# Two transformer blocks on one core: memory keys projected in float32, modulation sums placed behind steps, and 512-column weight chunks

## The chip, the cores and the metric

The kernel runs on one core of a Trainium2 chip. The metric is the device time of one execution in microseconds (us); the runs shown are whole executions, and a profiled execution carries a trace beside its time. PE is the matmul engine, PEld its weight loads, DVE the vector engine, ACT the scalar engine, POOL the GpSimd engine, SP the engine whose queue issues most loads.

## The reference, cut to what matters

The input `x` has 512 tokens of 1024 columns, all in float32. Two blocks follow one another, and beside them lies a memory of 256 rows.

```python
# block 1
mod = silu(c) @ w_ada + b_ada; shift, scale, gate = split(mod, 3)
h = rms_norm(x, g_pre) * (1 + scale) + shift
qa, ka, va, fa, za, qb, kb, vb, zb = split(h @ w_in)
oa = forgetting_attention(qa, ka, va, fa + b_fgate) * silu(za)      # 8 heads of 64, "fox"
ob = window_sink_attention(rope(qb), rope(kb), vb, sinks) * silu(zb)  # window 128, 2 key heads, "swa"
x = x + gate * rms_norm(concat(oa, ob) @ w_out, g_post)
# block 2
h = rms_norm(x, norm_g); mem_h = rms_norm(mem, mem_norm_g)
glu, cgate, dq, dk, dv, dg, xq, xg, merge = split(h @ w_in_2)
y = sig(m0)*conv_branch(glu, cgate) + sig(m1)*diff_attention(dq, dk, dv, dg) \
    + sig(m2)*memory_attention(xq, xg, split(mem_h @ w_mem_kv, 2))
x = x + y @ w_out_2
```

The memory attention norms its keys per head of 256 and multiplies by a gain; only `mem`, not `x`, enters keys and values.

## The kernel before, in words

The Python program is unrolled into one list of instructions for each engine. A planner orders it: it takes instructions by priority (`low(by)` moves a priority, `after(a, b)` puts one behind another on its engine), looks for those that its own timing holds to be ready, and lets a tile be written when a buffer of its tag is free. So a load on SP can wait for a buffer, and what comes behind it in SP's queue waits too.

**Matmuls in two halves.** Operands are split into a rounded part and a rest: `load_w` (L160) loads a chunk of 256 columns and 1024 rows in two loads of 512 KB, ACT casts each of four pieces of 512 elements a partition into `wh` (L169), and DVE subtracts it from the raw weights to give `wl` (L171); the last of four pieces goes to POOL. Four `wh` and four `wl` buffers, each half a chunk, hold two chunks. The tokens stand the same way in `hh` and `hl`. Three matmuls (high-high, high-low, low-high) then stand for one. `mm_T` (L190) streams 512 tokens against stationary weights; `mm_N` (L199) streams 256 weight columns against stationary tokens, 128 tokens `t` at a time.

**The opening** (L325 to L419). The memory is loaded and transposed on PE into `mh` and `ml` (L350 to L355). Then a loop runs over the eight chunks of `w_mem`: four for the keys `mk`, four for the values. In between, the tokens are loaded (L379, in the buffers that the memory leaves), normed and transposed (L386 to L392), and eight modulation sums run: `gemv_load` (L310) loads 1 MB into one of two `ada` buffers, `gemv` (L317 to L320) multiplies and adds on DVE in nine operations into `acc` (two buffers), and `ada(k)` sums it over the partitions by two tiny matmuls (L367), adds on DVE (L368, L369), and makes `hh[k]` and `hl[k]` on ACT and POOL (L371 to L373). `ADA_LOAD` and `ADA_DO` name the chunk at which each is loaded and done. The rotary angles (L424 to L436, sine tables on ACT) and some small constants (L439 to L451) are bound behind the last modulation sum. At a lower priority (`LOWMK`) the memory keys are normed (L457 to L463), transposed by 16 transposes (L468), and stored as `kT_d` (L472).

**After it.** w1c (264 columns: window keys, window values, forget gates) and qb0 are projected at once; everything else is cut into generators ("units" end at a `yield`) that `Fill` hands out between steps of attention: `staged` runs scores, transposes and values of an attention as a pipeline, and calls for `k` units after each step. The window stage takes zb0, qb1, zb1, va0, qk0 and za0; the fox stage qk1, va1, gate, qk2, za1 and qk3. Then come w_out (two halves of the tokens, each over four chunks), the second block with `ORDER2` as the list of its units, the depthwise convolution on DVE (L904), the cross stage with the memory (`xkv`, L1085, reads `kT_d` and `v_d`), the three branches, and w_out2 in four chunks. PSUM has three `mm` banks.

## Time and profile before

| | us |
|---|---|
| runs shown | 1193.62, 1193.22, 1196.0 (median 1193.62) |
| profiled execution, its own time | 1196.61 |
| its span, first to last instruction | 1194.8 |
| PE busy | 1154.0 |
| DVE busy | 926.6 |
| ACT busy | 551.7 |
| POOL busy | 213.3 |
| mean granted PE clock | 0.991 |

The busy time of PE counts a matmul from its start to its modelled end, and matmuls overlap, so the distance from start to start is the cost of one in a dense stretch. The granted clock (PEclk) is 1.00 at 2.4 GHz and 0.50 at 1.2 GHz. An idle time of an engine is followed by the engine and line that ended it.

### The profile page before, as it was taken

To read this page: it belongs to the slowest core of one execution; us is meant where nothing else is said; L and a number is where in the kernel's file an instruction comes from. 1 tells how busy PE (TensorE), PEld (TensorE's weight loads), DVE (VectorE), ACT (ScalarE), POOL (GpSimd) and SP (SyncE) were. 2 spreads that over 40 slices of the span, in tenths; PEclk is the share of its full clock that TensorE was granted. 3 is DMA by queue.
4 is the path that set the end of the run, shared out by engine and by line. 5 is a ranking of instruction groups with operands and counts; after the bars stand their busy time and mean duration, and the time that the engine had idled before them with its cause. 6 is when DMAs were issued, how large, how long until landed. Compare 5 with 4: busy or idle time off the path is not lost.

```text
span 1194.8 us, 18995 instructions
## 1 busy us (share of the span) xinstructions
PE 1154.0 (97%) x6960; PEld 1015.9 (85%) x6960; DVE 926.6 (78%) x2055; ACT 551.7 (46%) x1173; POOL 213.3 (18%) x161
## 2 busy tenths in 40 slices
PE   7879999999989999999999999999999999999998
PEld 6878887878889988998999887988888888888898
DVE  6997777898686699999989999999692596543341
ACT  7646566557554354445554452544422354232230
POOL 1334200000112211120111221221010132011020
PEclk9989999999999999999999999999999999999999
DMA  8765312443463423324233343333446755433232
GB/s 336 259 212 164 105 56 87 152 148 110 150 231 131 124 71 98 106 89 115 89 116 106 124 141 106 106 116 106 152 147 227 267 186 185 132 97 101 86 123 79
DMA packets 61965, 165.43 MB, mean 138 GB/s; under 512 B 7120, under 2 KB 15568, under 8 KB 60848
## 3 DMA queue, kind: packets, MB, share of 16 engines
q1 hardware_dynamic: 36560, 122.41, 32.5%
q10 hardware_dynamic: 25312, 41.82, 10.0%
q8 instruction: 55, 0.90, 0.3%
q14 instruction: 38, 0.31, 0.1%
HBM read 136.80 MB, written 20.58 MB: 132 GB/s over the span
## 4 chain that ended last, share of the span: by engine, by line
PE 63%; DVE 24%; issue 3%; ACT 1%; DMA 0%; POOL 0%; ACTq 0%; DVEq 0%; POOLq 0%
PE mm L190 40%; PE mm L199 15%; DVE cv L904 7%; DVE wl L171 3%; DVE dp L1025 1%; PE pv L773 1%; DVE dp L1032 1%; PE tp L751 1%; DVE dp L1031 1%; DVE ptl L754 1%; PE sc L1157 1%; PE pv L694 1%; PE pv L1200 1%; DVE qs L259 1%; PE tp L266 1%
## 5 line engine op out<-in xcount | busy, mean ns | idle before, releaser
L169 ACT CAST wh<-raw 128x512 fp32r<-128x512 f32 x372 | 215.3, 620 | 217.7 <-PE mm L190 96.2
L171 POOL TENSOR_TENSOR wl<-raw,wh 128x512 fp32r<-128x512 f32 (+1 forms) x93 | 141.8, 1525 | 831.9 <-ACT wh L169 668.8
L171 DVE TENSOR_TENSOR wl<-raw,wh 128x512 fp32r<-128x512 f32 (+1 forms) x279 | 201.7, 747 | 95.3 <-ACT wh L169 94.9
L190 PE MATMUL mm<-hh,wh 128*128 128x512 f32 x640 | 255.9, 400 | 0.0
L190 PE MATMUL mm<-hh,wl 128*128 128x512 f32 x640 | 251.8, 393 | 0.0
L190 PE MATMUL mm<-hl,wh 128*128 128x512 f32 x640 | 251.7, 393 | 0.0
L199 PE MATMUL mm<-wh,hh 128*128 128x256 f32 (+1 forms) x672 | 193.5, 289 | 0.2 <-ACT hh L824 0.2
L904 DVE SCALAR_TENSOR_TENSOR cv<-u,vec,cv 128x512 f32<-128x512 f32 x240 | 191.1, 796 | 3.4
L199 PE MATMUL mm<-wl,hh 128*128 128x256 f32 (+1 forms) x672 | 190.7, 284 | 0.3 <-POOL wl L171 0.3
L199 PE MATMUL mm<-wh,hl 128*128 128x256 f32 (+1 forms) x672 | 190.8, 284 | 0.0
L190 PEld LDWEIGHTS mm<-hh,wl 128*128 128x128 f32 x640 | 120.5, 188 | 27.0
L190 PEld LDWEIGHTS mm<-hh,wh 128*128 128x128 f32 x640 | 120.6, 188 | 24.7
L190 PEld LDWEIGHTS mm<-hl,wh 128*128 128x128 f32 x640 | 120.8, 189 | 24.5
L199 PEld LDWEIGHTS mm<-wl,hh 128*128 128x128 f32 x672 | 128.5, 191 | 0.8 <-POOL wl L171 0.6
L199 PEld LDWEIGHTS mm<-wh,hh 128*128 128x128 f32 x672 | 127.9, 191 | 0.8 <-ACT hh L824 0.5
L199 PEld LDWEIGHTS mm<-wh,hl 128*128 128x128 f32 x672 | 128.3, 191 | 0.0
L190 PE MATMUL mm<-bh,wh 128*128 128x512 f32 x192 | 75.9, 396 | 0.0
L190 PE MATMUL mm<-bh,wl 128*128 128x512 f32 x192 | 75.4, 393 | 0.0
L190 PE MATMUL mm<-bl,wh 128*128 128x512 f32 x192 | 75.4, 393 | 0.0
L1027 ACT ACTIVATE dp<-dp,dst 128x128 f32<-128x128 f32 (+3 forms) x64 | 35.5, 556 | 54.8 <-DVE dst L1025 54.6
L199 PE MATMUL mm<-wl,mh 128*128 128x256 f32 x128 | 39.3, 307 | 6.5 <-DVE wl L171 6.5
L190 PEld LDWEIGHTS mm<-bl,wh 128*128 128x128 f32 x192 | 36.1, 188 | 8.4 <-issue 0.2
(326 smaller groups left out, 2122.4 us busy)
## 6 DMA issues: line engine op xcount, KB each, us to landing
raw<-in_w_dram SPq DMA_DIRECT2D x120, 512.0 KB
raw<-in_w_out_dram SPq DMA_DIRECT2D x24, 512.0 KB
raw<-in_w_mem_dram SPq DMA_DIRECT2D x16, 512.0 KB
ada<-in_w_ada_dram SPq DMA_DIRECT2D x8, 1024.0 KB
ada<-in_w_gate_dram SPq DMA_DIRECT2D x8, 512.0 KB
k<-ks SPq DMA_DIRECT2D x32, 128.0 KB
o_d<-sph ACTq DMA_DIRECT2D x16, 256.0 KB
o_d<-spl ACTq DMA_DIRECT2D x16, 256.0 KB
```

The costliest lines, as they stand in the source:

```text
L169: act.copy(out=wh[:, s], in_=raw[:, s])
L171: eng.tensor_tensor(out=wl[:, s], in0=raw[:, s], in1=f(wh[:, s]), op=ALU.subtract)
L190: m = pe.matmul(out=ps, lhsT=a[:, c0:c0 + P], rhs=at(b, k), start=(n == 0 and i == 0), stop=(n == KT - 1 and i == 2))
L199: pe.matmul(out=ps, lhsT=at(a, k)[:, t * P:(t + 1) * P], rhs=b[:, 0:n], start=(start and m == 0 and i == 0), stop=(stop and m == len(order ...
L259: dve.scalar_tensor_tensor(out=s[b], in0=ps[a], scalar=sc, in1=f(s[a]), op0=ALU.mult, op1=ALU.subtract)
L266: pe.transpose(out=ps[:, t * P:(t + 1) * P], in_=src[:, t, c0:c0 + P], identity=ident)
L694: pe.matmul(out=pv4[0:64], lhsT=l_, rhs=r_[:, j], start=(cnt == 0), stop=(cnt == 3 * nk - 1))
L751: pe.transpose(out=tp[:, j * P:(j + 1) * P], in_=pt_[:, j * P:(j + 1) * P], identity=ident)
L754: dve.tensor_tensor(out=ptl[:, 0:n + 1, n * P:w], in0=tv, in1=f(pth[:, 0:n + 1, n * P:w]), op=ALU.subtract)
L773: pe.matmul(out=pv[0:64, j * P:], lhsT=l_, rhs=r_[:, j, j * P:], start=(j == 0 and i == 0), stop=(j == NT - 1 and i == 2))
L904: dve.scalar_tensor_tensor(out=a, in0=u[:, j:j + S], scalar=dw[:, m * 31 + j:m * 31 + j + 1], in1=a, op0=ALU.mult, op1=ALU.add)
L1027: act.activation(out=p_[:, :w], in_=p_[:, :w], func=AF.Exp, scale=-1.0, bias=st_[:, 0, n, m:m + 1], accum_out=st_[:, 1, n, m:m + 1])
```

## The change

- `load_w` can load 512 columns: four loads of 512 KB with two row blocks `k` each, eight pieces of one `k`; `wh` and `wl` have eight buffers of half the old size; `on_pool` names the pieces of four that POOL subtracts. `mm_W` is the loop over such a chunk: `k` outside, the tokens of two (or one) PSUM banks inside, with a `yield` after every second `k`.
- qb, va, dq with dk (as dqk), xq, w_out, w_out2 and the memory's value columns become chunks of 512. The rest stays at 256.
- The opening is a straight list: loads of the memory, the first key chunk and the tokens (each in buffers of its own); rotary angles; memory transposes into one float32 tile `mT`; the first key chunk (`mem_k`, plain float32 operands, one matmul instead of three, no split); token norm and transposes; the second key chunk; `mT` split into `mh` (ACT) and `ml` (POOL) in the tokens' old buffer; two value chunks (`mem_v`, half of the `wl` pieces on POOL). Each `ada(k, step)` is bound behind a step of PE: `steps` holds one matmul for each `k` of these four chunks, 0 to 31.
- The small constants get a raised priority. The memory keys are no longer transposed there; they are stored as `k_d`, and `xkv` transposes them, four transposes for a head, two ACT evictions with the gain and two DVE operations in place of one POOL operation.
- qb is projected whole before the window stage; the window stage takes zb0, zb1, qk0, za0 and za1, the fox stage va (both halves), qk1, gate, qk2 and qk3. The second xq chunk covers heads 2 and 3, `cross_pro(1)` comes ahead of the cross stage, which calls for four units after its first two steps.

The diff, cut to its core:

```diff
-    def load_w(src, w=CW, rp=None):
-        halves = []
-        for q in range(2):
-            raw = rp.tile([P, 4, w], F32, tag="raw", name="raw", bufs=4) if rp else wp.tile([P, 4, w], F32, tag="raw", name="raw", bufs=3)
-            nc.sync.dma_start(out=raw, in_=src[:, 4 * q:4 * q + 4, :])
-            wh = wp.tile([P, 4, w], F32R, tag="wh", name="wh", bufs=4)
-            wl = wp.tile([P, 4, w], F32R, tag="wl", name="wl", bufs=4)
...
+    def load_w(src, w=CW, rp=None, order=None, on_pool=(3,)):
+        kq = 4 if w == CW else 2
+        got = {}
+        for n, q in enumerate(order or range(KT // kq)):
+            raw = rp.tile([P, kq, w], F32, tag="raw", name="raw", bufs=4) if rp else wp.tile([P, kq, w], F32, tag="raw", name="raw", bufs=3)
+            nc.sync.dma_start(out=raw, in_=src[:, kq * q:kq * q + kq, :])
             for j in range(2):
-                s = slice(2 * j, 2 * j + 2)
-                act.copy(out=wh[:, s], in_=raw[:, s])
-                eng = pool if q and j else dve
-                eng.tensor_tensor(out=wl[:, s], in0=raw[:, s], in1=f(wh[:, s]), op=ALU.subtract)
-            halves.append((wh, wl))
-        return [(halves[k // 4][0][:, k % 4, :], halves[k // 4][1][:, k % 4, :]) for k in range(KT)]
+                h = kq // 2
+                s = slice(h * j, h * (j + 1))
+                wh = wp.tile([P, h, w], F32R, tag="wh", name="wh", bufs=8)
+                wl = wp.tile([P, h, w], F32R, tag="wl", name="wl", bufs=8)
+                act.copy(out=wh, in_=raw[:, s])
+                eng = pool if (2 * n + j) % 4 in on_pool else dve
+                eng.tensor_tensor(out=wl, in0=raw[:, s], in1=f(wh), op=ALU.subtract)
+                for k in range(h):
...
+
+    def mm_W(banks, w, xh, xl, ts, order=range(KT), n=NW):
+
+        for m, k in enumerate(order):
+            wh, wl = w[k]
+            for ps, t in zip(banks, ts):
+                for i, (a, b) in enumerate(((xh, wh), (xh, wl), (xl, wh))):
+                    pe.matmul(out=ps, lhsT=at(a, k)[:, t * P:(t + 1) * P], rhs=b[:, 0:n], start=(m == 0 and i == 0), stop=(m == KT - 1 and i == 2))
+            if m % 2 and m < KT - 1:
+                yield
...
-        mt = pa.tile([P, 2, 1024], F32, tag="nat2", name="mt")
...
+        xn = pa1.tile([P, NT, 1024], F32, tag="xn", name="xn")
...
+        def raw_chunk(c, qs):
+            for q in qs:
+                r = pa.tile([P, 2, NW], F32, tag="rawm", name="rawm", bufs=6)
+                nc.sync.dma_start(out=r, in_=A["w_mem"][c][:, 2 * q:2 * q + 2, :])
+                raws[c].append(r)
...
         for t in range(2):
             nc.sync.dma_start(out=mt[:, t, :], in_=A["mem"][t])
...
+        raw_chunk(0, range(4))
+        for t in range(NT):
+            nc.sync.dma_start(out=xn[:, t, :], in_=A["xn"][t])
...
+        pf = pa1.tile([P, NT], F32, name="pf")
+        dve.tensor_copy(out=pf, in_=posi)
...
+        act.activation(out=sn, in_=ang, func=AF.Sin)
+        act.activation(out=cn, in_=rn, func=AF.Sin, scale=-1.0, bias=halfpi)
...
-                act.activation(out=mh[:, k + j, :], in_=pj, func=AF.Copy, scale=g)
-                dve.scalar_tensor_tensor(out=ml[:, k + j, :], in0=pj, scalar=g, in1=f(mh[:, k + j, :]), op0=ALU.mult, op1=ALU.subtract)
...
+                if j:
+                    dve.tensor_scalar(out=mT[:, k + j, :], in0=pj, scalar1=g, scalar2=None, op0=ALU.mult)
+                else:
+                    act.activation(out=mT[:, k + j, :], in_=pj, func=AF.Copy, scale=g)
...
+        def mem_k(c):
+            banks = [mm_tile() for t in range(2)]
+            for k in range(KT):
+                for t in range(2):
+                    m = pe.matmul(out=banks[t], lhsT=mT[:, k, t * P:(t + 1) * P], rhs=raws[c][k // 2][:, k % 2, :], start=(k == 0), stop=(k == KT - 1))
+                steps.append(m)
+            for t in range(2):
+                act.activation(out=mk[:, t, c * NW:(c + 1) * NW], in_=banks[t], func=AF.Copy, scale=mrs[:, t:t + 1])
+
+        def mem_v(c, w):
+            banks = [mm_tile() for t in range(2)]
+            for k in range(KT):
+                for t in range(2):
+                    for i, (a, b) in enumerate(((mh, w[k][0]), (mh, w[k][1]), (ml, w[k][0]))):
+                        m = pe.matmul(out=banks[t], lhsT=a[:, k, t * P:(t + 1) * P], rhs=b, start=(k == 0 and i == 0), stop=(k == KT - 1 and i == 2))
+                steps.append(m)
...
+        def ada(k, step):
...
+                m = pe.matmul(out=pm[:, j:j + 1], lhsT=acc[:, j * P:(j + 1) * P], rhs=ones[:, 0:1], start=True, stop=True)
+                if j == 0:
+                    after(m, steps[step])
...
-        adas, marks = [], {}
-        for c in range(8):
-            w = load_w(A["w_mem"][c], rp=pa)
-            if c == 1:
-                load_x()
-            adas += [gemv_load(pa, A["w_ada"][k], 256, 2) for k in ADA_LOAD[c]]
-            for k in ADA_DO[c]:
-                ada(k)
...
+        load_ada(0, 1)
+        raw_chunk(1, range(4))
+        mem_k(0)
+        r = row_rstd(xn, NT)
+        for t in range(NT):
+            dve.tensor_scalar(out=xn[:, t, :], in0=xn[:, t, :], scalar1=r[:, t:t + 1], scalar2=None, op0=ALU.mult)
...
+            for t in range(NT):
+                pe.transpose(out=ps[:, t * P:(t + 1) * P], in_=xn[:, t, k * P:(k + 1) * P], identity=ident)
+            act.copy(out=xt[:, k, :], in_=ps)
+        load_ada(2, 3, 4)
+        wv0 = load_w(A["w_mem"][2], NW, on_pool=(1, 3))
+        load_ada(5, 6, 7)
+        mem_k(1)
+        mhl = pa1.tile([P, 2, KT, 256], F32R, tag="xn", name="mhl")
+        mh, ml = mhl[:, 0], mhl[:, 1]
+        for k in range(KT):
+            act.copy(out=mh[:, k, :], in_=mT[:, k, :])
+            pool.tensor_tensor(out=ml[:, k, :], in0=mT[:, k, :], in1=f(mh[:, k, :]), op=ALU.subtract)
+        ada(0, 10)
+        ada(1, 13)
+        mem_v(0, wv0)
+        ada(2, 16)
+        ada(3, 19)
+        ada(4, 22)
+        wv1 = load_w(A["w_mem"][3], NW, on_pool=(1, 3))
+        mem_v(1, wv1)
+        ada(5, 26)
+        ada(6, 29)
+        ada(7, 31)
...
-            after(dve.tensor_copy(out=pf, in_=posi), marks[ROTK])
...
-        after(first, marks[ROTK])
...
-            for k in range(0, KT, 2):
-                ps = tp_tile()
-                for j in range(2):
-                    for t in range(2):
-                        pe.transpose(out=ps[:, (2 * j + t) * P:(2 * j + t + 1) * P], in_=mk[:, t, (k + j) * P:(k + j + 1) * P], identity=ident)
...
-                nc.scalar.dma_start(out=kT_d[:, k:k + 2, :], in_=ko)
+                nc.scalar.dma_start(out=k_d[:, t, :], in_=mk[:, t, :])
...
+    def va_gen(pools):
+        w = w1n("va")
...
+            yield from mm_W(banks, w, hh, hl, (2 * tp, 2 * tp + 1))
...
-            w = w1(f"qb{c}")
-            nat = sw.tile([P, NT, CW], F32, tag="natq", name="natq", bufs=2)
+        def qb_gen():
+            w = w1n("qb")
...
+                yield from mm_W(banks, w, hh, hl, (2 * tp, 2 * tp + 1))
...
         fill.add("zb0", z_gen("zb0", 4))
-        fill.add("qb1", qb_gen(1))
         fill.add("zb1", z_gen("zb1", 6))
-        fill.add("va0", va_gen(0, fa))
         fill.add("qk0", qk_gen(0, fa))
         fill.add("za0", z_gen("za0", 0))
+        fill.add("za1", z_gen("za1", 2))
...
 
         fill.until("zb0")
         staged([(g, n) for g in range(2) for n in range(NT)], swa_sc, swa_tp, swa_pv, 1, 2)
-        fill.until("za0")
+        fill.until("qk0")
+        fill.until("za1")
...
+        fill.until("va")
...
+    fill.add("va", va_gen((fa, fb)))
     fill.add("qk1", qk_gen(1, fb))
-    fill.add("va1", va_gen(1, fb))
     fill.add("gate", gate_row())
     fill.add("qk2", qk_gen(2, fa))
-    fill.add("za1", z_gen("za1", 2))
     fill.add("qk3", qk_gen(3, fb))
...
-                ws = [load_w(A["w_out"][2 * cp + c]) for c in range(2)]
+                ws = load_w(A["w_out"][cp], NW, order=(2, 3, 0, 1) if hf + cp == 0 else None)
...
+                run(mm_W(pt_, ws, oh, ol, (2 * hf, 2 * hf + 1), order=oorder if hf + cp == 0 else range(KT)))
...
+        def nat_raw(w, dst):
...
+                banks = [mm_tile() for t in range(2)]
+                yield from mm_W(banks, w, hh, hl, (2 * tp, 2 * tp + 1))
...
-                yield from nat_raw((w2("dq", g), qn), (w2("dk", g), kn))
-            else:
-                yield from nat_raw((w2("dq", g), qn))
-                yield from nat_raw((w2("dk", g), kn))
-            nat_norm([qn, kn], 64, "dn")
...
+            qkn = dp.tile([P, NT, NW], F32, tag="qkn", name="qkn", bufs=1)
+            yield from nat_raw(w2n("dqk", g), qkn)
+            nat_norm(qkn, 64, "dn")
+            D["dqk", g] = qkn
...
-            nc.scalar.dma_start(out=kr, in_=kT_d[:, 2 * hd:2 * hd + 2, :])
+            nc.scalar.dma_start(out=kr, in_=k_d[:, :, hd * 256:(hd + 1) * 256])
...
-                act.copy(out=a, in_=src)
-                pool.tensor_tensor(out=b, in0=src, in1=f(a), op=ALU.subtract)
...
+            ps = tp_tile()
+            for j in range(2):
+                for t in range(2):
+                    pe.transpose(out=ps[:, (2 * j + t) * P:(2 * j + t + 1) * P], in_=kr[:, t, j * P:(j + 1) * P], identity=ident)
...
+                pj = ps[:, j * 256:(j + 1) * 256]
+                act.activation(out=a[:, j, :], in_=pj, func=AF.Copy, scale=gxqk[:, j:j + 1])
+                dve.scalar_tensor_tensor(out=b[:, j, :], in0=pj, scalar=gxqk[:, j:j + 1], in1=f(a[:, j, :]), op0=ALU.mult, op1=ALU.subtract)
...
+            if hd == 1:
+                add("xq", 1)
+                fill.first(("xq", 1))
...
+        cross_pro(1)
...
-        for c in range(4):
-            w = load_w(A["w_out2"][c])
...
+        for c in range(2):
+            w = load_w(A["w_out2"][c], NW)
+            cc = slice(c * NW, (c + 1) * NW)
+            for ts in (((0, 1), (2, 3)) if c == 0 else ((0,), (1,), (2,), (3,))):
...
+                run(mm_W(banks, w, yh, yl, ts))
```

## Rows read from the trace of the kernel before

**Rows 1.** The page, part 1: span, and PE's busy time.
```profile
span 1194.8 us, 18995 instructions
...
PE 1154.0 (97%) x6960; PEld 1015.9 (85%) x6960; DVE 926.6 (78%) x2055; ACT 551.7 (46%) x1173; POOL 213.3 (18%) x161
```

**Rows 2.** Opening by stretches: length; PE, PEld, DVE, ACT, POOL busy; clock, DMA, GB/s.
```profile
0.00:81.70 81.70, 64.58 (x460) 61.06 (x460) 69.34 (x162) 49.28 (x94) 24.12 (x18) 0.92 0.77 280
11.30:24.10 12.80, 12.80 (x99) 12.78 (x98) 11.35 (x36) 9.17 (x19) 3.58 (x2) 1.00 1.03 418
29.50:43.10 13.60, 13.22 (x96) 13.02 (x97) 13.57 (x23) 7.75 (x15) 6.19 (x4) 0.87 0.60 210
43.10:68.30 25.20, 20.18 (x162) 19.11 (x161) 24.78 (x52) 15.12 (x28) 10.59 (x6) 1.00 0.84 284
68.30:81.70 13.40, 9.93 (x56) 9.34 (x56) 11.49 (x29) 4.81 (x9) 3.55 (x2) 0.62 0.53 208
81.70:100.00 18.30, 16.59 (x121) 16.09 (x121) 16.95 (x55) 12.75 (x28) 9.31 (x13) 0.91 0.60 173
```

**Rows 3.** PE's waits from 0 to 100: total, times, longest.
```profile
PE mm L199 <- DVE wl L171: 6.5, 6, 1.8
...
PE mm L350 <- DVE ml L355: 1.7, 1, 1.7
PE tp L468 <- DVE mk L463: 1.4, 1, 1.4
```

**Rows 4.** Later stages by stretches, columns as in group 2.
```profile
130.00:210.00 80.00, 79.03 (x478) 66.81 (x477) 62.36 (x189) 51.54 (x140) 10.21 (x13) 1.00 0.23 71
390.00:740.00 350.00, 339.44 (x2208) 307.85 (x2208) 330.36 (x773) 162.36 (x359) 63.68 (x38) 1.00 0.35 107
740.00:900.00 160.00, 159.88 (x854) 136.89 (x854) 141.97 (x228) 68.05 (x139) 25.49 (x17) 1.00 0.37 124
```

**Rows 5.** PE alone in two dense stretches: 512-column and 256-column matmuls.
```profile
1080.00:1140.00 60.00, 60.00 (x259) 1.00 0.31 97
1152.00:1188.00 36.00, 36.00 (x304) 1.00 0.39 120
```

**Rows 6.** Timeline of PE, three places: start, duration, line, output and inputs.
```profile
24.05 4.17 PE L391 MATMUL mm<-cst,xn 128*128 128x128 f32 x32
...
81.39 0.50 PE L367 MATMUL sc<-cst,acc 128*128 128x1 f32 x4
81.75 0.37 PE L199 MATMUL mm<-wh,hh 128*128 128x264 f32 x1
...
111.11 2.32 PE L596 MATMUL tp<-cst,fz 128*8 128x512 f32 x8
113.36 0.33 PE L266 MATMUL tp<-cst,natk 128*128 128x128 f32 x1
```

**Rows 7.** Groups of DVE by form from 0 to 83: busy, mean ns.
```profile
L171 DVE TENSOR_TENSOR wl<-raw,wh 128x512 fp32r<-128x512 f32 x24 | 19.9, 860 | 0.0
...
L355 DVE SCALAR_TENSOR_TENSOR ml<-mm,vec,mh 128x256 fp32r<-128x256 f32 x8 | 3.5, 476 | 0.3 <-ACT mh L354 0.3
```

**Rows 8.** Waits of SP's queue from 0 to 140.
```profile
SPq L310 <- DVE acc L319: 34.6, 6, 7.7
```

**Rows 9.** ACT and POOL: token scaling, sine table, `hl`.
```profile
L371 ACT ACTIVATE ht<-xt,mod,gs 128x512 f32<-128x512 f32 x7 | 5.8, 827 | 8.3 <-DVE gs L369 6.1 <-DVE rv L210 2.3
...
87.68 1.28 ACT L435 ACT_TABLE_LOAD   x1
...
L373 POOL TENSOR_TENSOR hl<-ht,hh 128x512 fp32r<-128x512 f32 x6 | 9.3, 1558 | 14.8 <-ACT hh L372 14.0 <-DVE acc L319 0.8
```

**Rows 10.** Timeline: two `gemv` on DVE, and POOL beside the second.
```profile
46.72 2.46 DVE L319 SCALAR_TENSOR_TENSOR acc<-ada,cs,acc 128x256 f32<-128x256 f32 x6
...
63.18 3.50 DVE L319 SCALAR_TENSOR_TENSOR acc<-ada,cs,acc 128x256 f32<-128x256 f32 x6
...
64.76 3.04 POOL L373 TENSOR_TENSOR hl<-ht,hh 128x512 fp32r<-128x512 f32 x2 [3.03 <-ACT hh L372]
```

More of the change, by code (lines that the diff above doesn't have):

```diff
@@ L416, in two_block_kernel @@
-        for k in ADA_DO[8]:
-            ada(k)
+        load_ada(0, 1)
[5 more added lines that the diff above has]
+        for k in range(KT):
+            ps = mm_tile()
+            for t in range(NT):
+                pe.transpose(out=ps[:, t * P:(t + 1) * P], in_=xn[:, t, k * P:(k + 1) * P], identity=ident)
+            act.copy(out=xt[:, k, :], in_=ps)
@@ L444, in two_block_kernel @@
[L444 to L451 removed]
+            dve.tensor_scalar(out=nsink, in0=V("sinks"), scalar1=-1.0, scalar2=None, op0=ALU.mult)
@@ L642, in swa_sc @@
             if n == 0:
-                fill.until(f"qb{g}")
                 swa_q(g)
@@ L726, in fox_sc @@
         if n == 0 and m == 0:
-            fill.until(f"va{pr // 2}")
             fill.until(f"qk{pr}")
@@ L1130, in cross_pro @@
         def cross_pro(hd):
-            fill.until(("xq", hd))
-            qn = D["xq", hd]
+            fill.until(("xq", hd // 2))
+            qn = D["xq", hd // 2]
             qh = dp.tile([P, 2, S], F32R, tag="dvh", name="xqh")
@@ L1373, in _chunks, with _plain @@
     return out
-def _plain(w):
-    return _chunks(w, [np.arange(s, s + CW) for s in range(0, w.shape[1], CW)])
+def _plain(w, n=CW):
+    return _chunks(w, [np.arange(s, s + n) for s in range(0, w.shape[1], n)])
 def _layout(inp):
```

280 lines of the change are left out of this document (115 added, 165 removed).

## The prediction

> **What bounds the kernel now.** The page comes first: PE is busy 1154.0 of 1194.8 us, so what PE loses is some 41 us and the rest is PE's own work [rows 1]. Next, the table by stretch shows where it is lost. The eight memory chunks and the first projection (w1c) fill the time up to 100.0, and PE is busy 20.18 of 25.2 and 9.93 of 13.4 us in the stretches from 43.1 and 68.3, the second at a granted clock of 0.62 (between the levels of 1.2 and 2.4 GHz), while DVE is busy 24.78 of 25.2 just ahead of it [rows 2]. The waits name the cause: in the first 100 us PE waits 6.5 us for `wl` (the low halves that DVE cuts), 1.7 for `ml` and 1.4 for the scaled memory keys [rows 3]. Later, PE is busy 79.03 of 80, 339.44 of 350 and 159.88 of 160 us [rows 4]: there only PE's own work can be saved. So PE sets the end everywhere, and DVE feeds it too slowly in the opening.
>
> **What a column costs.** Between 1080 and 1140 there are 259 matmuls of 512 columns in 60 us (0.2317 us each), between 1152 and 1188 304 of 256 columns in 36 us (0.1184 each) [rows 5]. A pair of 256 costs 0.2368; one of 512 in its place saves 0.0051 us. By the Trainium skill's page "TensorE: Matmul & The Clock Gate", section "Back-to-back issue gap", a warm matmul costs its columns at 2.4 GHz plus some 2.5 ns, so the pair would save 2.5 ns and the term below would be 2.7 instead of 5.4 us; the rows show twice that, and I go by them. A float32 matmul leaves two records: eight records of 1280 columns in all take from 111.11 to 113.36 [rows 6], 2.25/1280 = 1.76 ns a column, 0.90 us for 512; I take 0.89, since the share per record weighs less at 512.
>
> **The opening as it is.** Ideal at those prices against measured [rows 2, 5]: chunks 0 and 1, 96 x 0.1184 = 11.4 against 12.8; chunks 2 and 3, 11.4 against 13.6; chunks 4 to 6, 17.0 against 25.2; chunk 7, 5.7 against 13.4; w1c, 96 matmuls, 11.4 against 18.3. Some 26 us above the ideal, of which a few are small sums and transposes.
>
> **What the change takes from DVE.** Key chunks lose their split: 16 chunk pieces of DVE go, 24 to 8 (the value chunks give half, not a quarter, to POOL), 16 x 0.860 = 13.8 us; 8 `ml` at 0.476 go to POOL, 3.8; one chain of ten small operations goes. Four evictions of `mT` come in. DVE does some 52 us ahead of w1c instead of 69.34 (my estimate from [rows 2, 7]); the rotary sums move to the very start, where the first loads are still under way. So PE, not DVE, should set the opening's length.
>
> **PE's new opening, step by step.** Memory transposes: first projection matmul at 11.3, as now (the 1.7 for `ml` goes [rows 3], but the sine table of 1.28 and two activations may come ahead on ACT [rows 9]: bounds 9.6 and 13.3). Keys 0, 16 float32 matmuls: 14.2, and 1.4 lost as in the stretch from 11.3 now, 26.9. Token transposes, 32 in 4.2 [rows 6], 31.1; their loads no longer stand behind a buffer. Keys 1: 14.2, 2.2 lost as in the stretch from 29.5 now, two modulation sums at 0.36 (81.39 to 81.75) [rows 6], 48.2. Values 0: 48 x 0.2317 = 11.1, three sums 1.1, a wait of 1 for the split, 61.4. Values 1: 11.1, two sums 0.7, a wait of 1.5, the last sum 0.4, 75.1. w1c: 11.4 and 1.5. That wait lies between 0 and 3.2 (two ACT operations of at most 0.827 and 1.558 for `hl` [rows 9], behind the last sum); 88.0. Both qb chunks at once: 96 x 0.2317 = 22.2, 110.2. Now the same work ends at 100.0 + 192 x 0.1184 = 122.7. **Gain 12.5.**
>
> What is given back: the 16 transposes of the memory keys move from there into the cross stage, 16 x 0.13 = 2.1, and PE is full there [rows 4]. The eight new operations of 0.476 on DVE [rows 7] lie beside PE's work (DVE 141.97 of 160 [rows 4]): nothing, or 3.8 if the cover is gone. The gate chunk za1 moves into the window stage and half of va out of it; PE's work is the same, and I set 1 for both points together (bounds 0 and 5).
>
> **Width elsewhere.** va, dqk, xq, w_out and w_out2 hold 192 + 768 + 384 + 384 + 384 = 2112 matmuls of 256 columns, 1056 pairs, x 0.0051 = 5.4. Splits and loads are as many bytes and pieces as before; larger rotary operations save a little DVE time beside PE: nothing.
>
> **Sum:** 12.5 - 2.1 + 5.4 - 1.0 = 14.8 us. The profiled execution took 1196.61, 2.99 above the median of the three runs (1193.62): 1181.8 there, 1178.8 for the median; **forecast 1179**. Own range: w1c's wait gone, the wait for values gone, clock never down after the transposes, no loss after, 8 us less: 1171; start at 13.3, the full 3.2 and twice the waits, 6 more: 1185.
>
> **Rivals.**
> A, loads behind gated sums. A modulation load waits for the `gemv` two before it (SP waits 34.6 us for this now, six times [rows 8]); the new order lets `gemv` k+2 begin only when sum k has passed its step on PE (two `acc` buffers). If SP keeps the written order, values 0 stand behind load 4, values 1 behind load 7. `gemv` has nine operations at 2.46/6 = 0.41 us [rows 10], 3.7 us, so load 4 goes out some 4 us after step 10 and value 0 is ready some 2.6 late; load 7 goes out 4 us after step 19, values 1 come 4.3 late, and at half the clock for a while 2.2 more: 9.1 instead of my 2.5, 6.6 us, **1185.6**. For: in the opening SP's order now is the written one. Against: a planner that sees the wait can pass it.
> B, the filler runs out: the window stage asks for 22 units of foreign work after its start, 16 are left instead of 20. If its last steps then run bare, up to four units of 2.7 us are lost: 10.9 less the 1 booked, **1189**, with a little of A 1191: no change. Against: PE, not DVE (62.36 of 80 us), fills that stretch [rows 4], and later matmuls can move up.
> C, **slower**: weights one chunk deep. A 512-column chunk holds all eight `wh`/`wl` pieces, so the next chunk's first piece is cut only when the second pass has begun; before, two chunks fitted. Where DVE's queue is full (330.36 of 350 us [rows 4]), PE then waits at the chunk's border for a cast, a queued operation and the split; at 0.860 us at most each [rows 7] that is 2.6, say 2.2 us, at 14 wide chunks: 31 us, **1179 + 31 = 1210**. It decides from 14.8/14 = 1.1 us a border on. Against: a freed piece has seven steps of 1.4 us until it is used.
> D, the new keys run at the lower clock throughout: 28 us more less the 3.6 booked, 1203. Against: the float32 stretch at 111.11 ran at full clock.
> The Trainium skill's page "SBUF — State Buffer", section "Who interferes with whom", speaks against the moves to POOL: a DVE operation with two SBUF inputs and a POOL one that reads SBUF exclude each other. The trace agrees in part: six sums of `gemv` take 2.46 us alone and 3.50 beside two `hl` on POOL [rows 10]. I book nothing for it: eight more POOL operations of half the width of `hl`, some 0.8 us each [rows 9], lie in DVE's slack, 52 of 75 us.
>
> **Chances.** Forecast 0.53, A 0.19, B 0.12, C 0.11, D 0.05. A measurement tells 0.3% (3.6 us) from no change: faster is below 1190.0, slower above 1197.2. So faster 0.72, same 0.12, slower 0.16. Range 1169 to 1193: it leaves out C, D and the ends.
>
> **What would show it.** Key matmuls in float32 at 0.44 us a record at clock 1.00; first w1c matmul near 75; PE busy above 0.9 from 43 on; the last qb matmul near 110; 512-column matmuls of va, dqk and w_out at 0.232. A would show as PE waiting for `wl` at values 1 with SP's `ada` issues just ahead; B as a PE gap before the first fox scores; C as waits for `wl` at dqk's borders. A first w1c matmul after 82 makes me wrong.

## The result: 1.1% slower, and the profile after

The changed kernel takes 1207.85 us (median of 4 runs, 1206.47 to 1212.31) against 1194.81 (4 runs, 1193.22 to 1197.01): ratio 1.0114, 95% interval 1.0082 to 1.0147, **13 us slower** where 16 faster were forecast. Its profiled execution took 1207.46. The page, part 1, beside [rows 1]:

```profile
span 1205.6 us, 16186 instructions
...
PE 1145.5 (95%) x5584; PEld 938.3 (78%) x5584; DVE 920.8 (76%) x2004; ACT 552.1 (46%) x1157; POOL 206.7 (17%) x158
```

PE's busy time fell by 8.5 us and the span rose by 10.8: PE waits more. The opening by stretches, with the columns of [rows 2]; the stretches end at the first value matmul, the first of values 1, the first of w1c, the first of qb and the last of qb:

```profile
0.00:49.00 49.00, 38.56 (x121) 20.27 (x121) 23.60 (x78) 23.52 (x46) 7.96 (x13) 1.00 0.75 288
49.00:63.70 14.70, 12.61 (x58) 9.75 (x58) 14.49 (x19) 9.29 (x16) 10.37 (x7) 1.00 0.43 144
63.70:84.30 20.60, 14.93 (x62) 11.13 (x62) 19.88 (x42) 11.35 (x19) 8.27 (x6) 0.92 0.78 269
84.30:104.60 20.30, 15.44 (x102) 15.02 (x102) 16.16 (x52) 8.04 (x20) 7.05 (x13) 0.83 0.61 212
104.60:126.80 22.20, 22.20 (x99) 17.91 (x99) 16.78 (x33) 10.53 (x20) 10.20 (x10) 1.00 0.43 135
```

DVE is busy 23.60 us of the first 49 and then 34.37 of 35.30: it stands idle first and is late afterwards. What PE waits for from 0 to 127 (total, times, longest), beside [rows 3]:

```profile
PE mm L405 <- DMA mt<-in_mem_dram: 6.0, 2, 5.6
PE mm L207 <- DVE wl L172: 4.9, 2, 2.9
PE mm L405 <- DVE mT L409: 3.9, 1, 3.9
PE sc L442 <- DVE acc L338: 3.5, 2, 2.8
PE mm L431 <- DVE wl L172: 3.1, 3, 1.3
PE mm L431 <- ACT wh L170: 1.2, 1, 1.2
```

The first line is the memory's load, 5.8 us in before too. Of the others that are shown, all but the last are waits for DVE. The timeline of DVE and POOL around the first sums shows why (start, duration; in brackets the idle time ahead and who ended it):

```profile
38.33 1.21 DVE L172 TENSOR_TENSOR wl<-raw,wh 128x512 fp32r<-128x512 f32 x1
48.72 0.16 DVE L445 SCALAR_TENSOR_TENSOR mod<-sc,vec 128x2 f32<-128x2 f32 x1 [9.19 <-PE sc L442]
...
49.31 0.69 DVE L172 TENSOR_TENSOR wl<-raw,wh 128x512 fp32r<-128x512 f32 x1
...
51.10 1.75 DVE L335 TENSOR_SCALAR acc<-ada,cs 128x256 f32<-128x256 f32 x2
52.77 2.95 DVE L337 SCALAR_TENSOR_TENSOR acc<-ada,cs,acc 128x256 f32<-128x256 f32 x2
...
49.32 3.12 POOL L172 TENSOR_TENSOR wl<-raw,wh 128x512 fp32r<-128x512 f32 x2 [5.92 <-ACT wh L170]
52.69 1.33 POOL L172 TENSOR_TENSOR wl<-raw,wh 128x512 fp32r<-128x512 f32 x1 [0.25 <-ACT wh L170]
53.97 1.47 POOL L450 TENSOR_TENSOR hl<-ht,hh 128x512 fp32r<-128x512 f32 x1
```

DVE waits 9.19 us for the first modulation sum, which PE takes only behind all of keys 1: "not before step 10" is a lower bound, and the sums rank behind the projection. Then POOL's splits start, and of the operations of `gemv`, six of which took 2.46 us alone [rows 10], two now take 2.95. SP's waits from 0 to 100, beside [rows 8]: what queues now are loads of weights (the values, then w1c and qb), behind splits, because three `raw` buffers are all there are; the modulation loads (L328) wait 19.2 us instead of 34.6.

```profile
SPq L164 <- DVE wl L172: 39.8, 9, 7.7
SPq L328 <- DVE acc L337: 9.7, 4, 3.2
SPq L328 <- DVE acc L335: 9.5, 2, 5.5
```

Behind the opening the table by stage tells more than any wait. The stages end at matmuls ahead of which both kernels have done the same projections. "Work" is PE's busy time at full clock (busy times granted clock, summed over slices of 3 us), "clock" the rest of its busy time, "waits" the stage less PE's busy time.

| stage | before | after | wide only | opening only |
|---|---|---|---|---|
| start to the last transposed `hn` (w_out) | 372.8 | 378.2 | 374.3 | 378.6 |
| to the last values of the difference heads | 344.5 | 348.0 | 348.5 | 344.6 |
| to the first matmul of w_out2 (cross, branches) | 427.5 | 432.1 | 430.9 | 429.2 |
| w_out2 | 46.1 | 43.7 | 43.7 | 46.4 |
| PE's work, clock, waits, whole | 1145.8, 8.1, 37.0 | 1133.4, 12.1, 56.5 | 1130.4, 13.1, 53.9 | 1144.3, 7.9, 46.6 |

(The last two columns are the first two experiments.) The change takes 12.4 us of work from PE and gives it 19.5 us of waits and 4.0 of clock. By the last qb matmul 4.1 us are lost (126.8 against the 122.7 worked out for before); the rest comes later, with PE's longest waits from 378 to 890 these:

```profile
PE tp L284 <- POOL xqn L987: 4.9, 1, 4.9
PE sc L1187 <- DVE xl L1119: 2.7, 1, 2.7
PE pv L1230 <- ACT xo L1233: 2.4, 2, 2.1
```

### The profile page after: what moved, and what is told of

Its sections match the earlier page's. It is cut to its first block, busy times and chain, and to the rows that moved or that the text cites. A ratio compares the mean times of both kernels' runs of the same rounds, so it can differ in the third digit from the quotient of the medians.

```text
span 1205.6 us, 16186 instructions
## 1 busy us (share of the span) xinstructions
PE 1145.5 (95%) x5584; PEld 938.3 (78%) x5584; DVE 920.8 (76%) x2004; ACT 552.1 (46%) x1157; POOL 206.7 (17%) x158
## 5 line engine op out<-in xcount | busy, mean ns | idle before, releaser
L170 ACT CAST wh<-raw 128x512 fp32r<-128x512 f32 (+1 forms) x360 | 214.9, 616 | 195.5 <-PE mm L198 115.0
L172 DVE TENSOR_TENSOR wl<-raw,wh 128x512 fp32r<-128x512 f32 (+1 forms) x266 | 194.1, 745 | 91.7 <-ACT wh L170 88.2
L215 PE MATMUL mm<-wh,hh 128*128 128x512 f32 x256 | 102.7, 401 | 0.6 <-ACT qkn L973 0.3
L215 PE MATMUL mm<-wh,hl 128*128 128x512 f32 x256 | 100.2, 391 | 0.0
L215 PE MATMUL mm<-wl,hh 128*128 128x512 f32 x256 | 100.1, 391 | 0.0
L215 PEld LDWEIGHTS mm<-wh,hh 128*128 128x128 f32 x256 | 48.2, 188 | 11.1 <-ACT qkn L973 1.0
L215 PEld LDWEIGHTS mm<-wh,hl 128*128 128x128 f32 x256 | 48.1, 188 | 10.4
L215 PEld LDWEIGHTS mm<-wl,hh 128*128 128x128 f32 x256 | 48.2, 188 | 9.1 <-DVE wl L172 0.3
L207 PE MATMUL mm<-wl,hh 128*128 128x256 f32 (+1 forms) x160 | 46.8, 293 | 4.9 <-DVE wl L172 4.9
L207 PE MATMUL mm<-wh,hl 128*128 128x256 f32 (+1 forms) x160 | 46.3, 290 | 0.0
```

The lines of the kernel that those rows point to most:

```text
L170: act.copy(out=wh, in_=raw[:, s])
L172: eng.tensor_tensor(out=wl, in0=raw[:, s], in1=f(wh), op=ALU.subtract)
L207: pe.matmul(out=ps, lhsT=at(a, k)[:, t * P:(t + 1) * P], rhs=b[:, 0:n], start=(start and m == 0 and i == 0), stop=(stop and m == len(order ...
L215: pe.matmul(out=ps, lhsT=at(a, k)[:, t * P:(t + 1) * P], rhs=b[:, 0:n], start=(m == 0 and i == 0), stop=(m == KT - 1 and i == 2))
```

## The experiments

Eighteen kernels were run; ratios are to the kernel before on the same chip. Two explanations stood against each other at the start: the new opening alone loses, by DVE's idle time and the splits that come late for it, and the wide chunks gain as forecast; or the wide chunks lose too, because DVE, not PE, sets the pace of the stages behind.

### Which half loses: e1 and e2

e1 puts the old opening back into the changed kernel; e2 puts the new opening into the kernel before (blocks exchanged whole, with `xkv` and the layout of w_mem that go with them). Both also carry the change's `load_w`: the weights' halves in eight small tiles, and w1c in four loads.

> The changed kernel with the opening of before put back (256-column memory chunks, split keys, key transposes in the opening, rotary sums late), and with the 512-column chunks and the new order of fillers everywhere else; w1c keeps its four loads. In the changed kernel's trace the last qb matmul ends 4.1 us later than the same work of before, and the whole span is 10.8 us longer, so 6.7 us are lost behind the opening. Theory 1 (the loss behind the opening belongs to the wide chunks and the cross stage): about 1194.8 + 6.7 - 2.1 (key transposes back in the opening) = 1199. Theory 2 (the wide chunks do save the forecast 5.4 us and what is lost later comes from the opening's disorder): about 1190. The gap of 4.9 us ahead of the third cross head's transposes stands by theory 1 and goes by theory 2.

> The kernel of before with the new opening alone (memory keys in float32, sums bound behind its steps, rotary angles first, keys transposed in the cross stage), all other chunks 256 columns wide and the old order of fillers. Theory 1 (half of the loss lies behind the opening and belongs to the wide chunks): 1194.8 + 4.1 + 2.1 = 1201. Theory 2 (all loss comes from the opening): 1207.9 + 5.4 = 1213. If the new opening gained 12.5 us as forecast, 1184.4.

e1: **1203.36**, ratio 1.0066 (1.0047 to 1.0086). e2: **1203.90**, 1.0075 (1.0055 to 1.0095). Both halves lose, 8.6 and 9.1 us; together they lose only 13. The wide half was forecast to gain 5.4, so the opening alone is not the cause. But the small tiles and the four loads of w1c are in both kernels: the two numbers part the opening from the wide chunks, and neither of them from the tiles (e9) or from the addresses (e17). How the 8.6 and the 9.1 divide was not measured.

### Who takes the width's gain: e5 and e6

```
-                for j in range(1, 31):
+                for j in range(1, 4):
```

once in before (e5), once in e1's kernel (e6).

> The kernel of before with 4 instead of 31 taps of the depthwise convolution: 27 x 8 = 216 operations of DVE at some 0.8 us, 173 us of DVE's work, are left out, and nothing of PE's. It is the measure for the next run. In the trace of before PE waits 19.5 us behind the opening. Both theories: 1195 less what of these waits hangs on DVE's queue, 1178 to 1190.

> The kernel of the first run (opening of before, 512-column chunks elsewhere), with the same 216 operations of the convolution left out. There, PE's busy time at full clock is 15.7 us less than in before, its waits 19.3 us more and the clock's price 5.3 us more. Theory 1 (DVE sets the pace from the windows to the cross stage, so what PE saves turns into waiting for DVE): with DVE freed the saving shows, and this is 6 to 14 us faster than the run with 4 taps and 256-column chunks. Rival (the wide chunks' own order makes the waits: two banks and eight weight pieces held for a whole chunk, a longer chain behind it): it stays slower than that run by 3 us or more.

e5: 1184.82. e6: **1176.14**. With DVE freed, wide chunks are 8.7 us faster (ratio of the medians 0.9927); with all taps they are 8.6 slower. Rows of the difference stage (columns of [rows 2]), first before and e1, then e5 and e6:

```profile
372.80:717.30 344.50, 336.47 (x2254) 308.17 (x2253) 318.73 (x754) 166.70 (x365) 62.44 (x38) 1.00 0.35 107
```
```profile
374.30:722.80 348.50, 335.50 (x1822) 288.32 (x1821) 322.88 (x745) 170.07 (x365) 62.74 (x39) 0.99 0.35 106
```
```profile
373.40:711.40 338.00, 334.29 (x2253) 308.22 (x2253) 248.02 (x642) 168.32 (x365) 59.27 (x39) 1.00 0.36 111
```
```profile
376.20:705.90 329.70, 328.66 (x1825) 286.36 (x1824) 243.58 (x632) 172.23 (x366) 58.76 (x39) 1.00 0.36 112
```

With all taps DVE is busy 318.73 of 344.50 us, and PE, with less work, waits 13.0 instead of 8.0. With four taps DVE has 90 us to spare, PE's waits shrink to 3.7 and 1.0, and the stage is 8.3 us shorter with the wide chunks. And e5 by itself, with PE's work as in before (1144.9 against 1145.8 us), is 11.4 us faster than before. So behind the opening DVE's queue, not PE, sets the pace, and the second explanation holds. Both differences take the wide chunks with their small tiles and w1c's four loads; whether width or tiles make e1's waits is not parted by them. (Both kernels leave out 27 of the convolution's 30 taps behind the first.)

### The weights' tiles: e7, e9, e10, e11

The change also keeps a chunk's halves in eight small tiles instead of four:

```
-            wh = wp.tile([P, 4, w], F32R, tag="wh", name="wh", bufs=4)
+                wh = wp.tile([P, h, w], F32R, tag="wh", name="wh", bufs=8)
```

e7 takes this and 512-column chunks in w_out and w_out2 into before; e9 takes the tiles alone; e11 is e7 with the old tiles; e10 is the changed kernel with four tiles of two pieces.

> The kernel of before with 512-column chunks only in the two output projections (w_out, w_out2), where no other chunks and no convolution run beside PE; the weights are held in pieces as in the changed kernel. From the stages of the first run: 58.7 to 54.9 us from the last head's values to the last transposed token, 46.1 to 43.7 us in the last stage. Theory 1 (the width pays where DVE has room): both stages shrink by about as much, 1194.8 - 6.2 = 1188.6. Rival (the shorter stages of the first run came from work that was merely moved out of them): 1193 to 1195.

> The kernel of before with one thing of the change alone: the weights' high and low halves are kept in eight tiles of half the size, each handed back by itself, and not in four tiles of two pieces. All chunks, operations, sizes and transfers stay as in before. The run with wide output projections lost 9.9 us behind hn's last transposes, 370.7 to 1152.7 instead of 372.8 to 1144.8, where its code differs from before in nothing else. Theory 1 (pieces handed back one by one let casts and splits go ahead of work that PE waits for): 1199 to 1205, with the loss in the difference and cross stages. Rival (the loss came from the shifted start of the stage, or from the order that happens to come out): within 2 us of 1195.

> The kernel of before with 512-column chunks in the two output projections alone, and the weights in four tiles of two pieces as in before. Theory 1 (the outputs' width pays, the single pieces cost): the difference and cross stages take what they take in before, 1194.8 - 3.8 = 1191, and the kernel beats both. Rival (it is the shifted stages, not the pieces): 1200 or more, as with single pieces (1202.6).

> The changed kernel with the weights in four tiles of two pieces as in before, everything else as changed. Theory 1 (half of the change's loss behind the opening is the handing back of single pieces): 1198 to 1202. Rival (the loss belongs to the width, whose chunk now holds all tiles; a wide chunk's next weights then wait even longer): 1208 or more.

e7: 1202.58, 1.0059 (1.0044 to 1.0074), a miss: the two projections shrink by 2.3 and 1.5 us, and two stages that hold no wide chunk grow by 10 (347.9 against 344.5 and 434.1 against 427.5). e9: **1206.22**, 1.0084 (1.0069 to 1.0099): the tiles alone cost 10 us. e11: **1194.61**, 0.9980 (0.9968 to 0.9992): with the old tiles the wide outputs gain. e10: 1207.10, 1.0091 (1.0076 to 1.0106): in the changed kernel the old tiles bring nothing that can be told from none, so there the tiles alone are not the cause. Difference and cross stage of before and of e9:

```profile
717.30:859.90 142.60, 139.95 (x778) 120.91 (x777) 129.19 (x223) 59.88 (x125) 25.38 (x16) 0.99 0.36 118
```
```profile
373.80:721.00 347.20, 336.36 (x2254) 307.52 (x2253) 320.65 (x754) 169.02 (x365) 62.00 (x39) 1.00 0.35 106
721.00:868.10 147.10, 141.63 (x778) 121.30 (x778) 130.72 (x223) 60.50 (x125) 24.61 (x16) 0.98 0.35 115
```

The counts are the same in both (2254 and 778 matmul records, 754 and 223 of DVE), and the stages are 2.7 and 4.5 us longer: the same work in another order. That the small tiles cost in this kernel is shown; that it is their earlier return, and how it makes the order worse, was not. It also shows that another order alone can cost as much as the effects that are looked for here, so a difference of a few us between two kernels is not pinned to one cause by its size.

### The second cross-query chunk: e8

```
-            nat_norm(qn, 256, "xn")
+            with low(-300):
+                nat_norm(qn, 256, "xn")
```

> The changed kernel with the norm of the cross queries (square, sum, ten small operations, scaling on POOL) raised in rank by 300. In its trace, the last matmul of the second cross-query chunk ends at 785.7 and the scaled chunk is there at 802.7, 17 us later, with convolution taps between each two of the ten small operations; PE waits 4.9 us for it. Theory 1 (a wide chunk puts two heads behind one chain, and the chain stands in DVE's queue): the chain shrinks by 4 us or more, the wait of 4.9 goes under 1, the time falls by 3 to 6 us to about 1203. Rival (the wait only moves to the next thing that is late): the wait goes and the time stays within 1.5 us of 1207.9.

1207.68, and the wait is still 4.9 us: each of the ten small operations waits for the one ahead, DVE has a tap or a split ready between most of them, and the rank changed nothing in that order. The edit did not do what it was meant to, so the theory about this one wait stays untested. Its opening, left as in the changed kernel, ends qb at 128.2 (126.8 there, 126.3 in e10): below, differences of 1.5 us at qb tell little.

### The opening, one cause at a time: e3, e12, e4, e13, e14

e3 raises the rank of a modulation sum (`pm`, its matmuls and `mod`):

```
+            with low(-300):
                 pm = sc_tile()
```

e12 does this, takes the binding away and gives `acc0` four buffers and `acc1` one:

```
-                if j == 0:
-                    after(m, steps[step])
```

e4 puts the rotary operations and the other small sums over the constants behind the last eviction of `mT`:

```
+        after(dve.tensor_copy(out=pf, in_=posi), mTd)
```

e13 takes the opening's splits from POOL, of both value chunks and of `ml`:

```
-        wv0 = load_w(A["w_mem"][2], NW, on_pool=(1, 3))
+        wv0 = load_w(A["w_mem"][2], NW, on_pool=())
...
-            pool.tensor_tensor(out=ml[:, k, :], in0=mT[:, k, :], in1=f(mh[:, k, :]), op=ALU.subtract)
+            dve.tensor_tensor(out=ml[:, k, :], in0=mT[:, k, :], in1=f(mh[:, k, :]), op=ALU.subtract)
```

e14 issues the first value weights ahead of three modulation loads:

```
-        load_ada(2, 3, 4)
         wv0 = load_w(A["w_mem"][2], NW, on_pool=(1, 3))
+        load_ada(2, 3, 4)
```

> The changed kernel with the modulation sums' matmuls and the operation that reads them raised in rank by 300, so that each stands at the step to which it is bound and not behind the whole projection. Theory 1 (the sums of modulation 0 and 1, ready at 27.7 and 30.7, are issued only at 48.2 behind all of keys 1; DVE waits 9.2 us for them from 39.5, and its later sums, the modulation loads 4 and 5 and the value weights behind these loads bunch up): the wait of 9.2 goes to under 3, the first w1c matmul comes at 76 to 79 instead of 84.3, and the time falls by 5 to 8 us, to about 1201. Rival (DVE and POOL hinder each other from 49 on, however early the sums are): the first w1c matmul at 82 or later, the time within 2 us of 1207.9.

> The changed kernel with the modulation sums' matmuls raised in rank by 300, bound behind no step, and with four accumulators for them (the second, helping, accumulator goes from two to one). In the changed kernel DVE waits 9.2 us from 39.5 on for the first two sums; with the rank raised but the binding kept it still waited 9.8 us, since the binding itself holds the sum until 40.2. Theory 1 (binding and two accumulators hold DVE's sums, and so the loads behind them): DVE's wait is under 2, the last qb matmul ends by 122 instead of 126.8. Rival (the opening's second half is bound by DVE and POOL, which stretch each other's operations, and the sums only come at another place): the last qb matmul ends at 125 or later.

> The changed kernel with the rotary angles and the small constants bound behind DVE's last eviction of the transposed memory. Theory 1 (DVE's queue stood still for the loads of positions and constants, until 7.1 and 9.1, ahead of the evictions that PE waits for): the wait of 3.9 us at 9.0 falls under 1, the first key matmul comes at about 10.3 instead of 13.8, and the time falls by some 3 us to 1205. Rival (the opening's later half hangs on DVE's sums and the loads behind them, not on PE's start): the first key matmul comes earlier and the first w1c matmul still comes at 83 to 85; the time within 1 us of 1207.9.

> The changed kernel with the opening's splits of value weights and of the memory on DVE alone, none on POOL (8 ml and 8 wl go over to DVE). In the changed kernel's trace, from 49.9 to 58.9, DVE's sums take 1.1 to 1.5 us each beside POOL's splits and 0.35 to 0.48 alone, and a split of 128x512 takes POOL 1.46 us, DVE 0.68. Theory 1 (each operation on POOL holds DVE up for about as long as it runs, so the moved splits cost DVE more than if it did them itself): the last qb matmul ends 3 to 8 us earlier than 126.8, at 119 to 124. Rival (DVE is the bound and gets 9.2 us more work, or the loads behind the modulations are the bound): 127 or later.

> The changed kernel with the first value weights' loads issued ahead of modulation loads 2 to 4 and not behind them (two lines change places). In the changed kernel three of the four loads of values 0 stand behind modulation loads that wait for their buffers. Theory 1 (loads behind gated loads, the forecast's rival A): PE's waits for the value weights' halves at 55.1 and 59.4 (1.3 and 0.8 us) go, those in values 1 shrink, and the last qb matmul ends 2 to 4 us earlier than 126.8. Rival (DVE's time, not the loads, is the bound): within 1 us of 126.8.

| run | first w1c matmul | end of qb | time, ratio |
|---|---|---|---|
| after | 84.3 | 126.8 | 1207.85, 1.0114 |
| e3 sums raised | 90.0 | 125.1 | 1208.36, 1.0105 (1.0082 to 1.0128) |
| e12 sums free | 100.7 | 134.2 | 1214.26, 1.0157 (1.0137 to 1.0177) |
| e4 rotary late | 80.2 | 124.2 | 1207.37, 1.0090 (1.0060 to 1.0121) |
| e13 no splits on POOL | 78.3 | 123.2 | 1207.36, 1.0097 (1.0075 to 1.0120) |
| e14 value loads first | 84.4 | 128.3 | 1208.73, 1.0113 (1.0093 to 1.0133) |

e3 left DVE's wait as it was, since step 10 itself ends at 40.2 (my expectation of under 3 us overlooked this):

```profile
DVE mod L446 <- PE sc L443: 11.6, 3, 9.8
```

e12 took the binding away, and the opening grew by 7 us: more modulations went ahead on DVE, beside the `ml` splits on POOL, and the first value weights were split at 51.33 and not at 38.33. But DVE still waited 6.91 us for the first sum, where I had expected under 2:

```profile
35.73 0.16 DVE L444 SCALAR_TENSOR_TENSOR mod<-sc,vec 128x2 f32<-128x2 f32 x1 [6.91 <-PE sc L443]
```

So taking the gate away does not help; what the wait itself costs e12 does not show. e4's step came as expected, the first key matmul at 9.94 instead of 13.82:

```profile
9.94 3.44 PE L432 MATMUL mm<-rawm,mT 128*128 128x512 f32 x4
```

but only 2.6 of these 3.9 us arrive at qb. e13 is the largest, 3.6 us: although DVE does sixteen more operations, its splits now take 0.64 us each, two in a row, where POOL took 1.33 to 1.56 in the timeline above:

```profile
50.02 1.29 DVE L172 TENSOR_TENSOR wl<-raw,wh 128x512 fp32r<-128x512 f32 x2
...
51.83 1.28 DVE L172 TENSOR_TENSOR wl<-raw,wh 128x512 fp32r<-128x512 f32 x2
53.03 0.87 DVE L337 SCALAR_TENSOR_TENSOR acc<-ada,cs,acc 128x256 f32<-128x256 f32 x2
```

The two `gemv` operations take 0.87 here and 2.95 in the changed kernel. e14 alone is a miss (it moves the loads of the first value chunk, not of the second). None of the five takes more than 0.5 us off the changed kernel's time: what e4 and e13 gain by qb is given back behind it.

### Three edits together, and with wide outputs: e15, e16

e15 is e4, e13 and e14 in one. e16 has e15's opening, w_out and w_out2 wide, four tiles of two pieces, all else as in before.

> The changed kernel with the two edits above together and the rotary angles and small constants behind the memory's evictions (that alone brought the first key matmul from 13.8 to 9.9 and the last qb matmul from 126.8 to 124.2). Theory 1 (the three losses of the opening stand one behind the other): the last qb matmul ends at 113 to 118, PE's waits for halves in both value chunks are under 2 us together, and the time falls by about as much, to 1196 to 1200. Rival (DVE's work ahead of w1c, some 60 us, sets the end however it is ordered): 121 or later, the time 1203 or more.

> The kernel of before with the opening of the run above, 512-column chunks in the two output projections alone, and the weights in four tiles of two pieces; keys are transposed in the cross stage. Theory 1 (the new opening gains once its three losses are mended, the outputs' width pays, the rest stays as in before): the wide outputs alone gave 1194.6; the opening gives 6 us and takes 2.1 for the transposes, 1188 to 1192, below both kernels. Rival (what the opening gains is given back where DVE sets the pace): 1193 or more.

e15: 1196.76, 1.0016 (0.9999 to 1.0032), 11 us below the changed kernel; qb ends at 115.9. The single gains at qb were 2.6, 3.6 and -1.5, together 10.9: with DVE free early, the loads that came first are split at once, six of them ahead of the first sum, for which DVE now waits 3.27 us (in the changed kernel DVE had cut one by then):

```profile
34.50 3.69 DVE L172 TENSOR_TENSOR wl<-raw,wh 128x512 fp32r<-128x512 f32 x6
```

Its opening by stretches (columns of [rows 2]), then its first w1c matmul in the timeline of PE:

```profile
0.00:49.00 49.00, 42.38 (x143) 24.04 (x144) 30.49 (x99) 29.74 (x57) 2.48 (x6) 1.00 0.81 314
49.00:74.50 25.50, 22.31 (x90) 17.52 (x89) 24.70 (x55) 12.35 (x22) 7.88 (x5) 0.87 0.69 249
74.50:93.80 19.30, 16.08 (x105) 15.54 (x105) 15.79 (x52) 8.78 (x21) 8.31 (x13) 0.82 0.63 226
```
```profile
74.55 0.63 PE L207 MATMUL mm<-wh,hh 128*128 128x264 f32 x2
```

e16: **1187.09**, 0.9933 (0.9913 to 0.9952), below both.

### Width or addresses: e17, e18

The work that left PE (15.4 us in e1) was three times the forecast, and the branches, with no wide chunk in them, took 209.5 us instead of 213.3 in every kernel that loads w1c in four parts. The traces hold no addresses. What e17 changes is the size of the largest tiles among the weights, and with it where the tiles lie:

```
-        for q in range(2):                       # raw, wh, wl: [P, 4, w]
+        kq = 4 if w == CW else 2
+        for q in range(KT // kq):                # raw, wh, wl: [P, kq, w]
```

> The kernel of before with w1c alone loaded in four parts of two k and not in two of four, as in the change. The largest weight tile of the pool then has 4096 bytes a partition (4 x 256 or 2 x 512 columns) instead of 4224 (4 x 264), so all later weights start at other addresses; nothing else differs. In all traces so far with tiles of 4096 or 2048 bytes the 512-column matmuls of the branches start 0.2267 us apart and the stretch from the first branch matmul to the first of the last projection takes 209.5 us, whatever the opening and the chunks; in all with 4224 or 2112 bytes 0.230 to 0.2335 and 213.1 to 214.2. Theory 1 (the addresses of the stationary weights set the matmuls' period): 0.2267 and 209.5 here too, and the time falls by 4 us or more, to 1184 to 1191. Rival (the wide chunks or the key layout shorten it): 0.2333 and 213.3, the time within 2 us of 1195.

> The mended kernel of the last run but one (new opening with its three losses mended, wide output projections, whole weight tiles; 1187.1) with w1c in four parts of two k, so that the largest weight tile has 4096 bytes a partition. Theory 1 (the period of the 512-column matmuls falls from 0.231 to 0.2267 us by the weights' addresses): the branches take 209.5 instead of 213.3, the last projection 43.7 instead of 44.4, the time 1176 to 1183. Rival (the period hangs on something else, or DVE's pace takes the gain): 1185 or more.

e17: **1192.14**, 0.9971 (0.9961 to 0.9982). e18: **1179.93**, 0.9873 (0.9854 to 0.9892), 16 us below before and 28 below the changed kernel. Matmuls of the branches in before, then in e17:

```profile
1100.27 0.39 PE L190 MATMUL mm<-hl,wh 128*128 128x512 f32 x1
1100.50 0.40 PE L190 MATMUL mm<-hh,wl 128*128 128x512 f32 x1
1100.74 0.39 PE L190 MATMUL mm<-hh,wh 128*128 128x512 f32 x1
```
```profile
1100.08 0.39 PE L192 MATMUL mm<-hh,wh 128*128 128x512 f32 x1
1100.31 0.39 PE L192 MATMUL mm<-hl,wh 128*128 128x512 f32 x1
1100.53 0.39 PE L192 MATMUL mm<-hh,wl 128*128 128x512 f32 x1
```

They start 0.23 to 0.24 us apart in before, 0.22 to 0.23 in e17; by thirds of the last 213 us ahead of w_out2 the mean is 0.2298 to 0.2333 in before and 0.2267 to 0.2271 in e17. e17 takes 4.5 us of PE's work away (1145.8 to 1141.3), with the same matmuls, so by the addresses as far as the edit shows; in e18 against e16, which differ in the same alone, it is 6.8 (1143.7 to 1136.9). Of e1's 15.4 us some 8.6 to 10.9 are left for the width, an estimate that takes the addresses to have done as much in e1.

## Why the prediction was wrong

The span came 25.6 us above the forecast (1205.6 against 1194.8 - 14.8 = 1180.0): 16.6 by the last qb matmul (126.8 against 110.2) and 9.0 behind it.

**The premise.** "So PE sets the end everywhere" is where it failed behind the opening. [rows 4] had DVE busy 330.36 of 350 us, and I used that row for a rival alone. e5 and e6 show it: with DVE freed the kernel before is 11.4 us faster with the same work on PE, and the same chunks give 8.7 us there and cost 8.6 without.

**Width elsewhere, 5.4.** The size of the term was off, and so was its sign on the path. The width took some 8.6 to 10.9 us of PE's work; over 1152 pairs (qb's 96 are in e1 too) that is 0.0075 to 0.0095 a pair and not 0.0051. The path got none of it: e1's PE waits 16.9 us more and pays 5.0 more for its clock (the text of e6 has 19.3 and 5.3; the table decides). In w_out2, where PE alone works, 2.4 us arrived, 1.7 of them at the old addresses (44.4 us in the trace of e11). The prediction's two prices are each a little low, since 259 and 304 count matmuls that reach over the ends of their stretch: from start to start it is 0.2333 and 0.1192, and the difference stays 0.0051.

**"Splits and loads are as many bytes and pieces as before"**, booked at nothing. The bytes were the same, the tiles were not. The eight small tiles cost 10 us in before (e9), and w1c in four parts gave 3.8 (e17). Neither was in the sum.

**"So PE, not DVE, should set the opening's length."** DVE did 58.0 us ahead of w1c, not 52, but 23.60 of them in the first 49 us, against 39 in before over the same time. The sums "at" their steps came behind the projection, and I took the binding for a place. Of the 16.6 us, 0.8 had arisen by the first value matmul, 1.5 arose in values 0, 6.9 in values 1 (20.6 against 13.7, with waits of 3.5 for the sums' `acc` and 2.2 for halves, and a clock of 0.92) and 7.4 in w1c.

**The start, 11.3 (bounds 9.6 and 13.3).** 13.82. I looked for what comes ahead of the evictions on ACT; it was DVE, whose raised rotary operations waited for the positions until 7.14 and for the constants until 9.12. e4 gives the 3.9 us back.

**"I book nothing for it"**, the exclusion of DVE and POOL. Taking the splits from POOL was worth 3.6 us by qb (e13), though nothing that can be told from none in that kernel's time (1207.36). The Trainium skill's page "SBUF — State Buffer", section "Who interferes with whom", says that a DVE operation with two SBUF inputs and a POOL one that reads SBUF exclude each other. This case agrees: two `gemv` operations in 2.95 us beside POOL, in 0.87 without. Idle time on DVE did not cover it, because it lay earlier.

**w1c, 11.4 and 1.5.** 20.3, with two waits for its low halves (4.9 us) and a clock of 0.83; still 19.3 in e15, with a clock of 0.82. Before had 18.3 at 0.91 [rows 2], and my 1.5 took neither over. No run mends this.

What held: keys 1 in 14.0 (14.2 forecast) and qb in 22.2 of 22.2 with PE never waiting. That e15's first w1c matmul comes at 74.55 (75.1 forecast) is luck: its values start at 43.56, 4.6 early, and values 1 take 18.9 us instead of 13.7.

**The rivals.** A's queue shrank (19.2 us of SP's waits are for modulation loads, 34.6 before), a new one for splits took its place (39.8), and moving the loads alone won nothing (e14). B came in small: from the matmuls of the forget gates' sums (126.8, in before 111.1) to fox's last values PE waits 5.9 us, in before 2.8, so 3.1 more and not 10.9. C's 1210 lies nearest to the measured time, but that is luck: from 378 to 726, where dqk is projected, PE waits 11.8 us in the trace, and none of it for a weight's half. D did not come, the keys ran at 1.00.

## What to carry to other kernels

Work that is saved on the busiest engine counts only in the stages where the next engine has room: read that stage by stage before pricing a saving, and test it by leaving out the other engine's work. A binding "not before step n" is no place in the order; the place comes from the rank. Where a shared buffer changes its size for one odd user (here 264 columns among 256), measure the matmuls that use the buffers behind it again.

## What the runs showed of the hardware

The period of float32r matmuls of 512 columns hung on the size of the largest weight tile, and so, as far as these runs show, on where the tiles lie: in the branches 0.2267 to 0.2271 us on average in all fourteen kernels with 4096 or 2048 bytes a partition, 0.2298 to 0.2333 in the six with 4224 or 2112. Which operand's address matters, and by which rule, was not tried.

In the changed kernel's opening a split of 128x512 took POOL 1.26 to 1.84 us and DVE 0.68 in six of ten cases, 1.21 to 1.79 in the four others, each of them beside an operation of POOL; two operations of `gemv` took 2.95 beside POOL and 0.87 without. There, where DVE was the late one, handing splits to POOL cost DVE more than doing them (e13, 3.6 us by qb).
